# Regrouping the first feed-forward layer of a fp32-exact hybrid trunk: 18 of 22 chunks folded, and weight quarters loaded anew

## The chip, the core and the metric

The kernel runs on one core of one Trainium2 chip. The core has a matrix engine (TensorE, PE in the profile, with PEld for its weight loads), a vector engine (VectorE, DVE), a scalar engine (ScalarE, ACT), GpSimd (POOL) and SyncE (SP), which here issues most of the transfers from the chip's main memory. The metric is device microseconds of one execution; smaller is better.

## What is computed

512 tokens of width 1024 go through two layers in fp32. Layer 0 mixes tokens with gated linear attention (GLA), layer 1 with a gated DeltaNet (GDN). Behind each mixer stands a gated feed-forward ("ConvFFN"), which this change is about. Each sublayer ends with `x = LayerNorm(alpha * x + f(x))`. The feed-forward is, in short:

```
up   = x @ w_in                      # 1024 -> 2 * 2816: gate half and value half
up   = causal_dwconv(up, conv_w)     # width 3 along the tokens
f(x) = (gelu(gate) * value) @ w_out  # 2816 -> 1024
```

The inner width 2816 is 22 chunks of 128 columns.

## The kernel before

**Products.** Every fp32 operand is split into a high part (a cast to the matrix engine's fp32r format) and a low part (the difference); a product is then three matmuls, high by high, high by low and low by high, which accumulate in a PSUM bank. The splitting is done by `split_out` (L690): the cast mostly on ACT, the difference on DVE.

**Up-projection ("fm").** Each chunk gives two items, gate and value; an item is one weight tile of 128 columns, 8 input chunks by 3 parts = 24 matmuls of 512 columns. The evacuation is the convolution: one pass of ACT (L978) and two of DVE (L980), then gelu on ACT for the gate or a multiply on DVE for the value.

**Down-projection.** It goes in groups of chunks, `GROUPS = ((0, 8), (8, 16), (16, 22))`, each directly behind the up-projection of its chunks. The first two groups are folded (function `folded`). A fold takes a pair of chunks by both halves of the model width by two halves of the 512 tokens as a 2x2 block product and does it with seven block products in place of eight: `FORMS` names the seven combinations of the activations (made on DVE in a tile `form`, then split into `fh` and `fl`), and the names b11, b21, t1, t2, b22, t3, t4 are the seven combinations of the weights' quarters. One weight item holds a name for two pairs (128x1024). Each name takes 2 halves x 3 parts = 6 matmuls of 512 columns per pair. A pair is thus 42 matmuls. In the plain form (`out_rows`, tile `tm`), two chunks by two width halves by four blocks of 128 tokens by 3 parts are 48. The last group of six chunks is plain, token block by token block, because each block of tokens is followed by its LayerNorm.

**Weights of a fold.** `fold_load` (L384) loads the quarters b11, b12 and b22 into tiles `b` (six of them, tag "folded") which stay for the whole fold, and b21 into the pool of three `raw` tiles. `issue_fold` makes the sums in place on DVE (L395): t1 = b11 + b12, t2 = t1 + b22, and so on; t3 = b12 + b22 is made in the b12 tile. SP issues each load as soon as its tile is free, in the order of the plan. Split weights go into a pool of four tiles `wh` and four `wl`.

**LayerNorm between the layers (`ln`, L834 to L875).** For each block of 128 tokens: the plain rows are added to the residual `h` (L638, DVE, once for each half of the width), statistics are taken (L639), the root is made on ACT, four tiny DVE operations follow, one half is normalised on DVE (L858) and the other on ACT (L857); PE transposes both halves (`xT`, 4 transposes each), ACT applies gain and bias in eight pieces (L867), and the result is split into `xh` (DVE at L871 for half 0, ACT at L874 for half 1) and `xl` (DVE, L875). The next layer's matmuls need the `xh` and `xl` of its tokens: in the first items after the feed-forward, of two token blocks at a time.

**Order.** All work is issued by a Python planner into the engines' queues. Each engine runs its queue in order. Weights are asked for a number of items ahead (`look`), and small generators such as `ln` are pushed between matmuls by a cost model of the planner.

**Names for the steps below.** `form` is a tile of 2048 columns of which two exist; `fh`/`fl` are four pairs of 1792 columns; in the last group these and the six "folded" tiles are reused as 36 pieces ("parts") for the plain group's activations and split weights.

Of the kernel before, what the change touches and what calls it, by code (L numbers as in the profile page):

```python
# [15 lines left out]
P = 128  # L16
# [12 lines left out]
            "t4": ("a22", 0)}  # L29
FOLD_NEW = {"b11": "b11", "t1": "b12", "t2": "b22", "b21": "b21", "t3": None, "b22": None, "t4": "b21"}  # L30
FOLD = [(n, FOLD_NEW[n], *FOLD_ALL[n]) for n in ("b11", "b21", "t1", "t2", "b22", "t3", "t4")]
GATED = (("b11", "a11", 0), ("b21", "a12", 1), ("t1", "w1", 1), ("t2", "v2", 0), ("b22", "v4", 1), ("t3", "v3", 0),
         ("t4", "a22", 0))
GATED_NEW = {"b11": "b11", "b21": "b21", "t1": "b12", "t2": "b22", "b22": "b22", "t3": "b11", "t4": "b21"}
# [32 lines left out]
def blk(i, n=P):  # L67
    return slice(i * n, i * n + n)


class Trunk:
# [190 lines left out]
    def plan_fold(self, w, f0, f1):  # L262

        group = {"w": w, "f0": f0, "m": (f1 - f0) // 2}
        for name, quarter, _, _ in FOLD:
            for i in range(0, group["m"], 2):
                self.plan.append(("fold", group, name, quarter, i))

# [99 lines left out]

    def fold_load(self, group, quarter, i):


        w, m = group["w"], group["m"]
        n = min(2, m - i)
        if quarter == "b21":
            t = self.rp.tile([P, 1024], F32, name=self.uid("raw"), tag="raw")
        else:
# [6 lines left out]
        group[quarter, i] = t  # L385

    def issue_fold(self, group, name, quarter, i):
        nc = self.nc
        n = min(2, group["m"] - i)
        cols = slice(0, n * S)  # L390
        get = lambda q: group[q, i]
        t = get({"b21": "b21", "t3": "b12", "b22": "b22"}.get(name, "b11"))
        other = {"t1": "b12", "t2": "b22", "t3": "b22", "t4": "b21"}.get(name)
        if other:
            nc.vector.tensor_add(t[:, cols], t[:, cols], get(other)[:, cols])  # L395
            self.vec(0.62 * n)
        self.held += 1
        wh = self.wp.tile([P, 1024], F32R, name=self.uid("wh"), tag="wh")
        wl = self.wp.tile([P, 1024], F32R, name=self.uid("wl"), tag="wl")
        self.split_out(wh[:, cols], wl[:, cols], t[:, cols])  # L400
        self.vec(0.62 * n)
        return [(wh[:, blk(j, S)], wl[:, blk(j, S)]) for j in range(n)]

    def gated_load(self, group, name, i):
# [4 lines left out]
        else:  # L409
            t = self.rp.tile([P, 1024], F32, name=self.uid("raw"), tag="raw")  # L410
        quarter = GATED_NEW[name]
        col = group["col"] + (2 - int(quarter[2])) * S
# [7 lines left out]
    def issue_gated(self, group, name, i):  # L420
        nc = self.nc
        t = group.pop((name, i))
# [11 lines left out]
        self.vec(1.24)  # L434
# [3 lines left out]
        self.split_out(wh, wl, t)  # L438
        self.vec(1.24)
        return [(wh[:, blk(j, S)], wl[:, blk(j, S)]) for j in range(2)]  # L440

# [10 lines left out]
    def load_ahead(self, until):  # L452
# [3 lines left out]
        while self.loaded < min(len(self.plan), until) and self.plan[self.loaded][0] in ("fold", "gated"):  # L456
            if self.plan[self.loaded][0] == "gated":
                self.gated_load(*self.plan[self.loaded][1:])
            else:
                _, group, _, quarter, i = self.plan[self.loaded]  # L460
                if quarter:
                    self.fold_load(group, quarter, i)
            self.loaded += 1
# [384 lines left out]
    def ln(self, tb, spill=False):  # L848
# [12 lines left out]
        for hf in range(2):  # L861
# [7 lines left out]
            xs = (slice(None), slice(4 * hf, 4 * hf + 4), blk(tb))  # L869
            if hf == 0:  # L870
                nc.vector.tensor_copy(self.xh[xs], c4(xf))  # L871
# [83 lines left out]

    def ffn_plan(self, w_in, w_out):
        for f0, f1 in GROUPS:
            for f in range(f0, f1):
# [24 lines left out]
    def ffn(self, cw, li, g, b, final, out=False):  # L983
        nc = self.nc
        self.stage(f"ffn{li}", FFN_SLOTS)
        fine = lambda: tuple(self.mp.tile([P, 1792], F32R, name=self.uid(n), tag=n, bufs=4) for n in ("fh", "fl"))
        for gi, (f0, f1) in enumerate(GROUPS):
            act, items, forms = {}, [], []
            last = gi == len(GROUPS) - 1
            if last:  # L990
                self.parts = [t[:, blk(i, S)] for _ in range(4) for t in fine() for i in range(3)]
                for _ in range(FOLDED):
                    t = self.mp.tile([P, 1024], F32, name=self.uid("b"), tag="folded", bufs=FOLDED)
                    self.parts += [t[:, blk(i, S)].bitcast(F32R) for i in range(2)]
            for f in range(f0, f1):
# [39 lines left out]
            if last:  # L1035
                self.drain()
                self.ln_begin(li, g, b)
                if out:
                    t = self.mp.tile([P, 2048], F32, name=self.uid("form"), tag="form", bufs=2)
                    self.ln_gb([t[:, blk(i, S)] for i in range(4)])  # L1040
# [6 lines left out]
    def folded(self, forms, first):  # L1047
# [5 lines left out]
        banks = [[self.psum("fold") for _ in range(2)] for _ in range(3)]  # L1053
        uses = [[n for n, _, _, at in FOLD if at == i] for i in range(3)]
        fresh = {(tb, hf) for tb in range(NTB) for hf in range(2)} if first else set()
# [16 lines left out]
        self.look = 3  # L1072
        for name, _, form, at in FOLD:
            f = FORMS.index(form) * 256
# [847 lines left out]
def kernel(  # L1922
# [24 lines left out]
    t.gdn_plan(gdn_w_in[0], gdn_w_out[0])  # L1947
    t.ffn_plan(ffn_w_in[1], ffn_w_out[1])
    t.hd = t.dp.tile([S, D], F32, name="hd", tag="hd")
# [45 lines left out]
```

## Time and profile before

| | |
|---|---|
| median of 3 runs | 1230.29 us (1230.27 to 1231.0) |
| profiled execution, its own time | 1230.9 us |
| its span, first to last instruction | 1229.2 us |
| PE busy | 1222.5 us (99%) |
| DVE busy | 933.8 us (76%) |
| ACT busy | 604.4 us (49%) |
| moved by DMA | 133.67 MB, mean 109 GB/s |

The first feed-forward lies at about 223 to 572 us of the span, the second at about 875 us to the end. In the first, the fold of chunks 0 to 7 runs at 307 to 347 us, that of chunks 8 to 15 at 433 to 472 us, and the plain rows at 537 to 572 us. In the profile's rows, `fm` is up-projection (and the mixers' input projections), `fold` is a folded down-projection, `tm` a plain one. `out<-in` names tiles without numbers.

### The profile page before, as it was taken

Reading aid. Unit: us, or ns where it says so; the run is one execution under the profiler, and the core shown is the slowest. Engines: PE = TensorE matmul, PEld = TensorE weight load, DVE = VectorE, ACT = ScalarE, POOL = GpSimd, SP = SyncE. Lnnn points to the kernel's source line nnn. Section 1 sums busy time; section 2 is a strip of 40 time slices with the busy share of each in tenths; the row PEclk is TensorE's granted clock in tenths of the full one; section 3 lists DMA queues with packets and bytes.
Section 4 is the critical chain, followed back from the end, with each engine's and each line's share of the span. In section 5 each row is a group of like instructions: output and inputs, shape, how many; then the busy total and the mean of one; then the engine's idle time right before and its main releaser. Section 6 shows DMA issues by size and latency. Waiting matters only on the chain.

```text
span 1229.2 us, 17198 instructions
## 1 busy us (share of the span) xinstructions
PE 1222.5 (99%) x6554; PEld 1030.8 (84%) x6554; DVE 933.8 (76%) x1535; ACT 604.4 (49%) x1070; POOL 123.1 (10%) x159
## 2 busy tenths in 40 slices
PE   9999999999999999999999999999999999999998
PEld 8888888988888888888988888988988888888886
DVE  4966986689957895666779975688589966796667
ACT  5654764544434443454678555634644434443440
POOL 4000000071000000001152030200053000000000
PEclk9999999999999999999999999999999999999999
DMA  7432253442453213433344351244352262223321
GB/s 207 117 104 69 86 170 105 144 132 69 131 160 92 63 59 115 118 103 106 97 136 128 97 135 42 77 130 138 120 154 70 69 204 87 88 83 103 105 67 69
DMA packets 171186, 133.67 MB, mean 109 GB/s; under 512 B 16390, under 2 KB 140362, under 8 KB 171104
## 3 DMA queue, kind: packets, MB, share of 16 engines
q1 hardware_dynamic: 166272, 123.62, 34.0%
q0 software_dynamic: 3872, 8.30, 2.2%
q8 instruction: 51, 0.84, 0.3%
q10 hardware_dynamic: 960, 0.66, 0.2%
q14 instruction: 31, 0.25, 0.1%
HBM read 126.77 MB, written 5.78 MB: 108 GB/s over the span
## 4 chain that ended last, share of the span: by engine, by line
PE 99%; DVE 1%; ACT 0%; issue 0%; DVEq 0%; POOL 0%; ACTq 0%; POOLq 0%
PE fm L205 54%; PE tm L205 20%; PE fold L205 15%; PE o L205 2%; PE xT L223 1%; PE pq L205 1%; PE pg L205 1%; PE vn L205 1%; PE yT L223 1%; PE V L205 0%; PE s L205 0%; PE qs L205 0%; PE ks L205 0%; PE ds L205 0%; PE sa L205 0%; PE warm L764 0%
## 5 line engine op out<-in xcount | busy, mean ns | idle before, releaser
L205 PE MATMUL fm<-xh,wh 128*128 128x512 f32 (+2 forms) x1104 | 401.8, 366 | 0.7 <-ACT xh L690 0.7
L205 PE MATMUL fm<-xl,wh 128*128 128x512 f32 (+2 forms) x1104 | 399.9, 365 | 0.0
L205 PE MATMUL fm<-xh,wl 128*128 128x512 f32 (+1 forms) x1080 | 392.8, 366 | 0.0
L690 DVE TENSOR_TENSOR wl<-raw,wh 128x1024 fp32r<-128x1024 f32 (+1 forms) x162 | 201.0, 1243 | 152.6 <-ACT wh L690 152.3
L690 ACT CAST wh<-raw 128x1024 fp32r<-128x1024 f32 (+1 forms) x163 | 168.8, 1037 | 226.4 <-PE fm L205 143.7
L205 PEld LDWEIGHTS fm<-xh,wh 128*128 128x128 f32 (+1 forms) x1104 | 206.9, 188 | 33.8 <-ACT xh L690 1.1
L205 PEld LDWEIGHTS fm<-xl,wh 128*128 128x128 f32 (+1 forms) x1104 | 206.9, 188 | 32.7
L205 PEld LDWEIGHTS fm<-xh,wl 128*128 128x128 f32 x1080 | 202.8, 189 | 33.0
L980 DVE SCALAR_TENSOR_TENSOR conv<-fm,ffn_cw,conv 128x511 f32<-128x511 f32 x112 | 83.5, 745 | 8.6 <-ACT conv L978 7.2
L205 PE MATMUL fold<-wh,fh 128*128 128x512 f32 x224 | 87.6, 391 | 0.0
L205 PE MATMUL fold<-wl,fh 128*128 128x512 f32 x224 | 87.4, 390 | 0.1
L205 PE MATMUL fold<-wh,fl 128*128 128x512 f32 x224 | 87.2, 389 | 0.0
L690 ACT CAST wh<-b 128x1024 fp32r<-128x1024 f32 x48 | 49.6, 1053 | 60.4 <-PE fold L205 25.5
L998 ACT ACTIVATE conv<-conv 128x512 f32<-128x512 f32 x44 | 27.8, 632 | 80.5 <-DVE conv L980 80.5
L890 POOL TENSOR_TENSOR h<-h,gb 128x512 f32<-128x512 f32 x16 | 28.1, 1776 | 334.5 <-DMA gb<-in_ln_g_dram 334.5
L690 DVE TENSOR_TENSOR wl<-b,wh 128x1024 fp32r<-128x1024 f32 x48 | 57.9, 1220 | 2.3 <-ACT wh L690 2.3
L1511 DVE SCALAR_TENSOR_TENSOR conv<-fm,gdn_cw,conv 128x511 f32<-128x511 f32 (+2 forms) x72 | 54.0, 790 | 3.2 <-ACT conv L1509 2.6
L205 PE MATMUL tm<-wh,xh 128*128 128x512 f32 x128 | 52.9, 414 | 0.0
L205 PEld LDWEIGHTS fold<-wh,fh 128*128 128x128 f32 x224 | 42.0, 188 | 9.8 <-DVE h L1069 1.2
L205 PE MATMUL tm<-wh,xl 128*128 128x512 f32 x128 | 50.2, 392 | 0.0
L205 PE MATMUL tm<-wl,xh 128*128 128x512 f32 x128 | 50.0, 391 | 0.0
L205 PEld LDWEIGHTS fold<-wl,fh 128*128 128x128 f32 x224 | 42.0, 188 | 9.4 <-DVE wl L690 0.9
(358 smaller groups left out, 1965.5 us busy)
## 6 DMA issues: line engine op xcount, KB each, us to landing
raw<-in_ffn_w_in_dram SPq DMA_DIRECT2D x88, 512.0 KB, 3.9
raw<-in_gdn_w_in_dram SPq DMA_DIRECT2D x32, 512.0 KB, 4.1
raw<-in_ffn_w_out_dram SPq DMA_DIRECT2D x28, 512.0 KB, 3.7
raw<-in_gla_w_in_dram SPq DMA_DIRECT2D x26, 512.0 KB, 3.7
b<-in_ffn_w_out_dram SPq DMA_DIRECT2D x24, 512.0 KB, 4.9
raw<-in_gla_w_out_dram SPq DMA_DIRECT2D x8, 512.0 KB, 3.9
raw<-in_gdn_w_out_dram SPq DMA_DIRECT2D x8, 512.0 KB, 4.0
h<-in_x_dram SPq DMA_DIRECT2D x8, 256.0 KB, 4.3
```

Source lines behind the costliest of these rows:

```text
L205: t = self.nc.tensor.matmul(out, a, b, start=start, stop=stop, skip_group_check=joined)
L223: t = self.nc.tensor.transpose(out, a, self.ident[:n, :n])
L690: return self.nc.scalar.copy(dst_h, src), self.nc.vector.tensor_sub(dst_l, src, dst_h)
L890: nc.gpsimd.tensor_mul(h[hf], h[hf], gb[hf])
L980: nc.vector.scalar_tensor_tensor(a[:, d:], ps[:, :S - d], tap(2 - d), a[:, d:], ALU.mult, ALU.add)
L998: nc.scalar.activation(a, a, AF.Gelu)
L1511: self.conv = nc.vector.scalar_tensor_tensor(a[:, d:], ps[:, :S - d], tap(3 - d), a[:, d:], ALU.mult, ALU.add)
```

## The change

- `GROUPS` becomes a table by layer. The first feed-forward has groups (0, 8), (8, 18), (18, 22): 18 chunks folded and four plain. The second keeps (0, 8), (8, 16), (16, 22).
- The six "folded" tiles are gone. Each of the seven names loads its own quarter when it is due: b11, and b22 of the first two pairs, into `gw` (4 tiles), the other ones into `raw` (3 tiles); where a group has an odd pair, its single-pair items go into small slots `fq`. So b11, b12 and b22 are loaded twice in a fold. The weights' sums are no longer taken from kept quarters: the first item of a pair, b11, becomes the running total in `gw`; t1 and t2 add into it, t3 is the total less the reloaded b11 and is made in `raw`, and t4 adds the reloaded b21 to the total. The same function (`issue_quarter`, adds at L402, L405 and L407) now serves the gated stage of the GLA layer, whose t4 is made in the total too, where it was made in `raw`.
- `form` has one tile, not two; `fh`/`fl` have five pairs, not four. The pieces for the plain group are 30, not 36; in the second feed-forward what does not fit is put into the six slots of the stage.
- In `ln` the cast of half 0 goes from DVE to ACT for token blocks 0, 1 and 2, in all three places where `ln` runs between layers. Block 3 keeps it on DVE.

The core of the diff (the group of `GATED` names, the unchanged lines and the moved `gated_load` are left out):

```diff
-FOLD_NEW = {"b11": "b11", "t1": "b12", "t2": "b22", "b21": "b21", "t3": None, "b22": None, "t4": "b21"}
+QUARTERS = {"b11": "b11", "b21": "b21", "t1": "b12", "t2": "b22", "b22": "b22", "t3": "b11", "t4": "b21"}
...
-GROUPS = ((0, 8), (8, 16), (16, 22))
+GROUPS = {False: ((0, 8), (8, 18), (18, 22)), True: ((0, 8), (8, 16), (16, 22))}
...
-FOLDED = 6
+PAIRS = 5
...
-    def fold_load(self, group, quarter, i):
+    def fold_load(self, group, name, i):
...
-        if quarter == "b21":
-            t = self.rp.tile([P, 1024], F32, name=self.uid("raw"), tag="raw")
+        if name == "b11" or name == "b22" and i == 0:
+            t = self.mp.tile([P, 1024], F32, name=self.uid("gw"), tag="gw", bufs=4)
+        elif n == 1:
+            t = self.slot("fq")
         else:
-            t = self.mp.tile([P, 1024], F32, name=self.uid(quarter), tag="folded", bufs=FOLDED)
+            t = self.rp.tile([P, 1024], F32, name=self.uid("raw"), tag="raw")
...
-        get = lambda q: group[q, i]
-        t = get({"b21": "b21", "t3": "b12", "b22": "b22"}.get(name, "b11"))
-        other = {"t1": "b12", "t2": "b22", "t3": "b22", "t4": "b21"}.get(name)
-        if other:
-            nc.vector.tensor_add(t[:, cols], t[:, cols], get(other)[:, cols])
...
         elif name == "t3":
             nc.vector.tensor_sub(t, total, t)
         elif name == "t4":
-            nc.vector.tensor_add(t, total, t)
-            del group["sum", i]
+            nc.vector.tensor_add(total, total, t)
+            t = group.pop(("sum", i))
...
-            if hf == 0:
+            if hf == 0 and tb == NTB - 1:
                 nc.vector.tensor_copy(self.xh[xs], c4(xf))
...
-        fine = lambda: tuple(self.mp.tile([P, 1792], F32R, name=self.uid(n), tag=n, bufs=4) for n in ("fh", "fl"))
+        fine = lambda: tuple(self.mp.tile([P, 1792], F32R, name=self.uid(n), tag=n, bufs=PAIRS) for n in ("fh", "fl"))
...
-                        t = self.mp.tile([P, 2048], F32, name=self.uid("form"), tag="form", bufs=2)
+                        t = self.mp.tile([P, 2048], F32, name=self.uid("form"), tag="form", bufs=1)
...
-        for name, _, form, at in FOLD:
+        for name, form, at in FOLD:
```

Three places show how instructions move. In them a name's number tells tiles apart; `h_99` and `h_100` are the two halves of token block 0, `h_101` and `h_102` of block 1, `h_103` and `h_104` of block 2, `h_105` and `h_106` of block 3. Line numbers of the changed kernel are lower by 1 on PE (L204 for L205, L222 for L223), and by 8 in much of the rest (L682 for L690, L630 for L638, L867 for L875).

PE in the plain rows of the first feed-forward, where the transposes of token block 0 stand. Before:

```order
L205 MATMUL tm_4611<-fl_4081,fl_4083 128x512
L205 MATMUL tm_4611<-fh_4082,b_4087 128x512 x3
L223 MATMUL xT_4631<-ident_86,h_99 128x128 x4
L223 MATMUL xT_4643<-ident_86,h_100 128x128 x4
L205 MATMUL tm_4663<-fl_4083,fh_4076 128x512 x3
L205 MATMUL tm_4663<-b_4084,fh_4076 128x512 x2
```

And now:

```order
L204 MATMUL tm_4712<-fh_4337,fl_4338 128x512
L204 MATMUL tm_4712<-fl_4338 128x512
L222 MATMUL xT_4719<-ident_86,h_99 128x128 x4
L222 MATMUL xT_4731<-ident_86,h_100 128x128 x4
L204 MATMUL tm_4712<-fh_4337,fl_4338 128x512
L204 MATMUL tm_4774<-fl_4332,fh_4331 128x512 x3
```

Before, they stood behind the third half row (`tm_4611` is block 1's first half), with 18 matmuls to a half row; now they stand ahead of the last of the 12 matmuls of the fourth half row (`tm_4712`, block 1's second half).

PE at the end of the same rows, with the transposes of block 2 (`h_103`, `h_104`) and the GDN layer's first matmuls (`fm`). Before:

```order
L205 MATMUL tm_4825<-b_4084,fl_4077 128x512
L223 MATMUL xT_4832<-ident_86,h_103 128x128 x4
L223 MATMUL xT_4844<-ident_86,h_104 128x128 x4
L205 MATMUL tm_4825<-b_4085,fl_4077 128x512 x3
L205 MATMUL tm_4825<-b_4086,fh_4078 128x512 x3
L205 MATMUL tm_4825<-b_4088,fh_4082 128x512 x2
L205 MATMUL tm_4825<-b_4088,fl_4083 128x512
L205 MATMUL tm_4825<-b_4089,b_4087 128x512 x3
L205 MATMUL fm_4913<-xh,wh_4659 128x256
```

And now:

```order
L222 MATMUL xT_4840<-ident_86,h_101 128x128 x4
L222 MATMUL xT_4852<-ident_86,h_102 128x128 x4
L204 MATMUL tm_4832<-fl_4334,fl_4338 128x512
L204 MATMUL tm_4874<-fh_4335,fh_4331 128x512 x4
L204 MATMUL tm_4874<-fl_4336,fh_4331 128x512
L204 MATMUL tm_4874<-fh_4335,fl_4332 128x512
L204 MATMUL tm_4874<-fh_4337,fl_4336 128x512 x3
L204 MATMUL tm_4874<-fh_4337,fl_4338 128x512
L204 MATMUL tm_4874<-fl_4338 128x512
L204 MATMUL tm_4874<-fh_4337,fl_4338 128x512
L222 MATMUL xT_4930<-ident_86,h_103 128x128 x4
L222 MATMUL xT_4942<-ident_86,h_104 128x128 x4
```

Between the transposes of blocks 1 and 2 there stand 13 plain matmuls now, where there were 36, and block 2's transposes come behind the last plain row, ahead of the first `fm`.

DVE ahead of block 2's normalisation (the last row of each piece makes `h_103`), from the add of block 2's second half. Before:

```order
L638 TENSOR_TENSOR h_104<-h_104,tm_4735 128x512
L875 TENSOR_TENSOR xl<-xf_4759,xh 128x4x128
L639 BN_STATS ln_st_773_4708<-h_104 128x6
L690 TENSOR_TENSOR wl_4800<-raw_4797,wh_4799 128x1024
L834 BN_AGGR ln_mv_4782<-ln_st_773_4708 128x2
L838 TENSOR_SCALAR ln_var_4786<-ln_mv_4782 128x1
L842 RECIPROCAL ln_rs_4788<-ln_root_4784 128x1
L843 SCALAR_TENSOR_TENSOR ln_t_4789<-ln_rs_4788,ln_var_4786 128x1
L844 SCALAR_TENSOR_TENSOR ln_rs_4788<-ln_t_4789,ln_rs_4788 128x1
L856 SCALAR_TENSOR_TENSOR ln_nb_4793<-ln_mv_4782,ln_rs_4788 128x1
L858 TENSOR_SCALAR h_103<-h_103,ln_mv_4782,ln_rs_4788 128x512
```

And now, from the statistics behind that add:

```order
L631 BN_STATS ln_st_797_4775<-h_104 128x6
L682 TENSOR_TENSOR wl_4829<-raw_4826,wh_4828 128x1024
L826 BN_AGGR ln_mv_4811<-ln_st_797_4775 128x2
L630 TENSOR_TENSOR h_105<-h_105,tm_4832 128x512
L830 TENSOR_SCALAR ln_var_4815<-ln_mv_4811 128x1
L834 RECIPROCAL ln_rs_4817<-ln_root_4813 128x1
L631 BN_STATS ln_st_812_4833<-h_105 128x6
L835 SCALAR_TENSOR_TENSOR ln_t_4818<-ln_rs_4817,ln_var_4815 128x1
L867 TENSOR_TENSOR xl<-xf_4845,xh 128x4x128
L836 SCALAR_TENSOR_TENSOR ln_rs_4817<-ln_t_4818,ln_rs_4817 128x1
L848 SCALAR_TENSOR_TENSOR ln_nb_4822<-ln_mv_4811,ln_rs_4817 128x1
L850 TENSOR_SCALAR h_103<-h_103,ln_mv_4811,ln_rs_4817 128x512
```

The add and the statistics of block 3's first half and one `xl` now stand inside the chain that makes block 2's normalisation.

More of the change, by code (lines that the diff above doesn't have):

```diff
@@ L437, in issue_gated, with gated_load @@
         wl = self.wp.tile([P, 1024], F32R, name=self.uid("wl"), tag="wl")
-        self.split_out(wh, wl, t)
-        self.vec(1.24)
-        return [(wh[:, blk(j, S)], wl[:, blk(j, S)]) for j in range(2)]
+        self.split_out(wh[:, cols], wl[:, cols], t)
+        self.vec(0.62 * n)
+        return [(wh[:, blk(j, S)], wl[:, blk(j, S)]) for j in range(n)]
+    def gated_load(self, group, name, i):
+        if name == "b11":
+            t = self.mp.tile([P, 1024], F32, name=self.uid("gw"), tag="gw", bufs=2)
+        else:
+            t = self.rp.tile([P, 1024], F32, name=self.uid("raw"), tag="raw")
+        quarter = QUARTERS[name]
+        col = group["col"] + (2 - int(quarter[2])) * S
+        c0 = 2 * i + int(quarter[1]) - 1
+        src = group["w"].rearrange("(c p) f -> p c f", p=P)[:, c0:c0 + 3:2, col:col + S]
+        load = self.nc.sync.dma_start(t.rearrange("p (j f) -> p j f", j=2), src)
+        if name == "b11":
+            self.behind(load, self.load)
+        group[name, i] = t
+    def issue_gated(self, group, name, i):
+        return self.issue_quarter(group, name, i, 2)
     def prefetch(self):
@@ L459, in load_ahead @@
             else:
[L460 to L462 removed]
+                self.fold_load(*self.plan[self.loaded][1:])
             self.loaded += 1
```

65 lines of the change are left out of this document (21 added, 44 removed).

## The prediction

> **What bounds the kernel now.** I read first the page's head with the busy times and the clock, then the waits of PE, then the chain of work that ended last, then single stretches. The page:
>
> ```profile
> span 1229.2 us, 17198 instructions
> PE 1222.5 (99%) x6554; PEld 1030.8 (84%) x6554; DVE 933.8 (76%) x1535; ACT 604.4 (49%) x1070; POOL 123.1 (10%) x159
> PEclk9999999999999999999999999999999999999999
> PE 99%; DVE 1%; ACT 0%; issue 0%; DVEq 0%; POOL 0%; ACTq 0%; POOLq 0%
> ```
>
> PE is busy for all but 6.7 us of the span (1229.2 less 1222.5), the clock is granted in full in all 40 slices, and the chain that ended last runs through PE for 99%. All of PE's named waits (engine and line, what released it, total, times, longest):
>
> ```profile
> PE warm L764 <- POOL one L97: 1.1, 1, 1.1
> PE fm L205 <- ACT xh L690: 0.7, 1, 0.7
> PE mid L205 <- ACT diag L906: 0.6, 1, 0.6
> ```
>
> So the time is the matmul stream. A matmul that goes saves its pitch; anything else costs only where it makes PE wait. But a busy PE here may also be a PE whose matmul was held a little, so I compare each stretch of the chain with its count times the free pitch. Chain, start, length, what:
>
> ```profile
> 346.72 86.59 PE fm L205 x382
> 433.30 32.64 PE fold L205 x144
> 466.40 5.61 PE fold L205 x24
> 307.68 19.27 PE fold L205 x85
> 326.97 13.69 PE fold L205 x59
> 341.11 5.61 PE fold L205 x24
> ```
>
> Both 86.59 / 382 and 32.64 / 144 are 0.2267 us: the free pitch of 512 columns. The second fold of the first feed-forward (433.30) is thus at full rate but for its last 24, which take 5.61 in place of 5.44. The first fold (307.68) is at full rate up to 326.97; there 59 matmuls take 13.69 in place of 13.38, so 0.3 us are lost at that place.
>
> **The change, part by part.**
>
> *Matmuls.* A pair of chunks is 42 matmuls folded and 48 plain. One pair changes sides: 6 x 0.2267 = 1.36 us less. There is no doubt about the count; it is 0.11% of the time. One measurement can tell about 0.2% (2.46 us) from no change.
>
> *Transfers and the reload chain.* Before, each quarter came once; now three come twice, 512 KB for two pairs. For eight chunks that is 6 loads, 3 MB, on four folds some 13 MB beside the 133.67 MB at a mean of 109 GB/s. The queue has room. What matters is the three `raw` buffers: 11 of a fold's 14 items now pass through them. These are the rows for one load of such a quarter (times, KB, median us to landing) and for DVE's work in the first fold:
>
> ```profile
> raw<-in_ffn_w_out_dram SPq DMA_DIRECT2D x28, 512.0 KB, 3.7
> b<-in_ffn_w_out_dram SPq DMA_DIRECT2D x24, 512.0 KB, 4.9
> 303.19 1.22 DVE L395 TENSOR_TENSOR b<-b,b 128x1024 f32<-128x1024 f32 x1
> 308.05 1.22 DVE L395 TENSOR_TENSOR b<-b,b 128x1024 f32<-128x1024 f32 x1
> 324.56 1.22 DVE L395 TENSOR_TENSOR b<-b,raw 128x1024 f32<-128x1024 f32 x1
> 325.69 2.35 DVE L690 TENSOR_TENSOR wl<-b,wh 128x1024 fp32r<-128x1024 f32 x2
> L690 ACT CAST wh<-raw 128x1024 fp32r<-128x1024 f32 (+1 forms) x163 | 168.8, 1037 | 226.4 <-PE fm L205 143.7
> 312.00:337.00 25.00, 24.98 (x110) 20.33 (x110) 24.97 (x31) 10.76 (x11) 0.00 (x0) 1.00 0.41 129
> ```
>
> The last row is the stretch 312 to 337 us: length, then busy time of PE, PEld, DVE, ACT and POOL, the clock, the DMA share, GB/s. DVE is full there, and PE's lost 0.3 us at 326.97 is the first of the two `wl` that start at 325.69, which ends at 326.9. A buffer's turn is the load 3.7, an add 1.13 (324.56 to 325.69), the ACT cast 1.04 and the `wl` 1.18 (half of 2.35): 7.05 us. Three buffers give an item every 2.35 us; PE takes one in 12 x 0.2267 = 2.72. So the loads keep pace as long as they land within 3 x 2.72 less 3.35 = 4.8 us. Singly issued loads are the row with 3.7; the 4.9 belongs to `b` tiles issued in a run while the queue is fullest, and the reloads are issued singly, each when DVE frees a buffer. I take 3.7: no stall.
>
> *The adds of a fold* stay eight for eight chunks. But the two b12 + b22 (303.19 and 308.05), which were made ahead of the fold, become "total less b11" inside it. Ahead of the `wl` at 325.69 there is then one add less net, 1.13 us, which is more than the 0.3 lost there; behind it the t3 and t4 items have less cover, about 1 us on my count of the queue. The first folds of both feed-forwards can gain 2 x 0.3 = 0.6. Bounds: -0.6, and +2.0 if two such items in each of the four folds come 0.25 us late. I take -0.3.
>
> *The fold of ten* has 21 items of 12 or 6 matmuls, 210 x 0.2267 = 47.6 us. Its DVE load per matmul is that of the second fold, which ran at 0.2267 throughout. The updates of `h` are as many as before. 0.
>
> *One `form` tile, five pairs.* The next pair's value convolution on ACT must wait until DVE has split the last one's form (128x1792, a single operation of 2 us); PE meanwhile has weights two items ahead, 2 x 24 x 0.2267 = 10.9 us of matmuls. 0.
>
> *The plain rows of the first feed-forward.* This is the place of the main cost. Before, chain and DVE groups of 536.7 to 572.4 us (times, busy us, mean ns), then some single rows of DVE and ACT:
>
> ```profile
> 536.83 12.48 PE tm L205 x54
> 549.31 0.95 PE xT L223 x8
> 550.27 9.56 PE tm L205 x42
> 559.83 0.87 PE xT L223 x8
> 568.88 0.87 PE xT L223 x8
> 569.76 2.77 PE tm L205 x12
> L639 DVE BATCH_NORM_STATS2 ln_st<-h 128x6 f32<-128x512 f32 x7 | 4.9, 694 | 0.2
> L690 DVE TENSOR_TENSOR wl<-raw,wh 128x1024 fp32r<-128x1024 f32 x4 | 4.8, 1208 | 0.0
> L638 DVE TENSOR_TENSOR h<-h,tm 128x512 f32<-128x512 f32 x7 | 4.8, 686 | 3.1 <-PE tm L205 3.1
> L875 DVE TENSOR_TENSOR xl<-xf,xh 128x512 fp32r<-128x512 f32 x5 | 3.5, 691 | 0.5 <-ACT xh L874 0.4
> L871 DVE CAST xh<-xf 128x512 fp32r<-128x512 f32 x3 | 1.3, 425 | 1.9 <-ACT xf L867 1.9
> 555.75 1.21 DVE L690 TENSOR_TENSOR wl<-raw,wh 128x1024 fp32r<-128x1024 f32 x1
> 556.88 0.20 DVE L834 BATCH_NORM_AGGREGATE ln_mv<-ln_st 128x2 f32<-128x12 f32 x1
> 558.24 0.54 DVE L858 TENSOR_SCALAR h<-h,ln_mv,ln_rs 128x512 f32<-128x512 f32 x1
> 552.73 0.62 ACT L874 CAST xh<-xf 128x512 fp32r<-128x512 f32 x1
> ```
>
> Before, PE loses some 0.4 us here: 54 matmuls at 0.2267 are 12.24, not 12.48, and three smaller differences. A block of tokens gives PE 36 matmuls and two transposes, 8.16 + 0.87 = 9.0 us; with four chunks it is 24 and two, 5.44 + 0.87 = 6.3. DVE's work for a block hardly shrinks: two adds and two statistics, 4 x 0.61 (a large operation starts 0.08 us ahead of the end of the one in front: 555.75 + 1.21 against 556.88); aggregate to normalisation 1.36 (556.88 to 558.24) and 0.54; two `xl` 1.22; one to two `wl` of the GDN weights at 1.13. With one that is 6.7 us of pure work, less some 0.25 us of waiting for the root into which other work now falls: 6.5 against PE's 6.3, before DVE waits once for PE. The cast that goes to ACT (0.42 from DVE, 0.62 onto ACT) helps and leaves the balance near zero.
>
> Following the new order row by row with these durations, from the end of the last `fm`: the transposes of block 0 stand behind 47 matmuls (10.65 us), but the normalisation is done at about 11.1: 0.4 us of wait. For block 1, PE comes 36 matmuls and one pair of transposes later, and DVE has two `wl`, two `xl`, three adds and three statistics to do in between, the first only when PE's interrupted half row is done: 0.5 us. For block 2, PE comes 13 matmuls and the transposes later, 2.95 + 0.87 = 3.8 us; DVE has statistics, `wl`, aggregate, add, statistics, `xl` and the tiny ones first (0.61 + 1.13 + 0.24 + 3 x 0.61 + 0.9 = 4.7) and 0.54 for the normalisation, 5.2 in all, about 0.3 of which passes while PE waits for block 1's second half on ACT: 1.1 us. Together 2.0 us, less the 0.4 lost before: +1.6. Bounds: -0.4 (none of these waits, and the old one gone) and +4 (each of three blocks late by a further `wl` and a half `xl`, some 0.8 us). If they stand, the next that is late are block 1's `xl` of half 1, which the first GDN matmuls need about 0.4 us after it is made.
>
> The Trainium skill says in VectorE: DVE Perf Modes, section on the DRAIN you can't avoid, that the next operation does not start before the pipeline of the last one has emptied. Read strictly, the 0.08 us of overlap would be gone, with some 16 large operations in these three chains 1.3 us more, and the sum below would come to 1231.5. The trace doesn't agree with that reading: 556.88 lies ahead of 555.75 + 1.21 = 556.96.
>
> *Start of these rows.* With all GDN weights cast ahead on ACT, the last chunk's convolution starts up to one cast (1.04) later; the new order puts 20 matmuls, 4.5 us, ahead of the first that needs it, and I find the two about equal. 0, bounds 0 and +0.8.
>
> *The same cast in the other two places where `ln` runs between layers:* a block there has 24 matmuls too and PE has no gap; the last operand comes about 0.5 us later with over 1 us to spare. 0. *Second feed-forward's tail and the GLA gated stage:* the operands move to other tiles, nothing joins the last chain. 0, at most 0.3 either way.
>
> **Sum:** -1.36 - 0.3 + 1.6 = -0.1 us. On the profiled execution (1230.9, span 1229.2) that is 1230.8; that execution lies 0.6 above the median of 1230.29, so against the median it is 1230.2.
>
> **Rivals.**
>
> *A: the saving alone arrives.* The planner's order hides the three waits, because DVE runs a little ahead (in the old rows it waited 3.1 us for `tm`, which is slack that I may have undercounted). Then -1.36 - 0.6 and at most the old 0.4: 1228.3 to 1228.0. For it speaks that no PE wait of this sort was named in the old trace; against it that PE's share of a block falls by 2.7 us and DVE's by 0.4.
>
> *B: the reloads come late (slower).* Place: t3 and t4 of each fold, five `raw` items in a row. Above a landing of 4.8 us each item is late by a third of the excess. At 6.0 us that is 0.4 x 5 x 4 folds = 8 us, less the cover of 1 us in each fold: +4, 1234.2. For it speak the 4.9 of the `b` row and a DMA share of 0.41 in the first fold; against it the 3.7.
>
> *C: the plain rows cost more.* Every block is DVE-bound by two `wl` in place of one; the upper end of +4: 1232.6.
>
> *D: the change does next to nothing,* because gain and cost cancel: that is the forecast itself.
>
> **Chances.** Forecast (waits of 0.8 to 2.5 us in the plain rows) 0.52; A 0.22; B 0.12; C 0.14. Below 1227.8 (faster by over 0.2%) only a quarter of A reaches, where other small holds go as well: 0.06. Above 1232.8 lie B and half of C: 0.19. Within 0.2%: 0.75. The range takes in A's value and C's: 1228.0 to 1233.2; it leaves out B and the ends of A and C.
>
> **What would show it.** In the new profile, `tm` and `fold` matmuls fall and rise by 48 and 42. In the chain, the plain rows of the first feed-forward would show pieces of `xT` with waits of DVE's normalisation (L850) ahead of them, in the order 0.4, 0.5, 1.1 us; without them A holds. The folds would each take 38.1 us at 0.2267, without the loss at the ninth item; if PEld waits for `wl` there, or DVE's adds wait for `raw`, B holds. I would be wrong altogether if PE waited in the fold of ten or ahead of a convolution for the single `form`.

## The result, and the profile after

| | before | after |
|---|---|---|
| median | 1230.52 us (7 runs, 1230.27 to 1231.18) | 1234.49 us (7 runs, 1233.58 to 1235.35) |
| profiled execution, its span | 1230.9, 1229.2 us | 1233.58, 1231.6 us |

The ratio is 1.003, 95% interval 1.002 to 1.004: the change costs 4.0 us, 0.32%, and the kernel's own runs spread over 1.8 us where they spread over 0.9 before. 1234.49 lies above the range of 1228.0 to 1233.2.

The page of the changed kernel: PE has 6 matmuls less and 1.0 us less busy time, and still the span is 2.4 us longer. What the chain of waits passes through has changed most.

```profile
span 1231.6 us, 17277 instructions
PE 1221.5 (99%) x6548; PEld 1028.8 (84%) x6548; DVE 936.7 (76%) x1536; ACT 611.2 (50%) x1081; POOL 122.0 (10%) x159
DMA packets 176003, 142.84 MB, mean 116 GB/s; under 512 B 16727, under 2 KB 140699, under 8 KB 175921
PE 81%; DVE 13%; issue 2%; ACT 2%; DMA 1%; DVEq 0%; ACTq 0%; POOL 0%; POOLq 0%
```

The DMA line says how much was really loaded anew: 142.84 less 133.67 is 9.2 MB, not the 13 MB of the prediction. Of the four quarters, b21 was loaded twice before the change as well, once for its own item and once for t4, and b12 still comes once. Only b11 and b22 come a second time now, so a fold of eight chunks has 14 loads of 512 KB where it had ten. (The text on the change, which says that b11, b12 and b22 are loaded twice, has this wrong.)

Before, 99% of that chain was PE. Now 13% of it is DVE and 1% is waiting for loads. PE's waits (engine and line, releaser, total, times, longest) name two new ones, besides one of 0.2 us:

```profile
PE fold L204 <- DVE h L1058: 2.2, 4, 0.8
PE xT L222 <- DVE h L850: 0.6, 1, 0.6
```

The first is new: inside the folds PE waits for DVE's update of `h`, since that update must have read the PSUM bank before the next name may write into it. How it comes to be late is read in DVE's timeline of the first fold (start, length, operation, and in brackets the idle time before it with its releaser):

```profile
327.19 2.35 DVE L682 TENSOR_TENSOR wl<-raw,wh 128x1024 fp32r<-128x1024 f32 x2
329.46 1.28 DVE L1056 SCALAR_TENSOR_TENSOR h<-h,fold 128x512 f32<-128x512 f32 x2
330.65 1.22 DVE L405 TENSOR_TENSOR raw<-gw,raw 128x1024 f32<-128x1024 f32 x1
333.27 1.23 DVE L407 TENSOR_TENSOR gw<-gw,raw 128x1024 f32<-128x1024 f32 x1 [1.40 <-DMA raw<-in_ffn_w_out_dram]
334.41 0.68 DVE L1058 TENSOR_TENSOR h<-h,fold 128x512 f32<-128x512 f32 x1
335.01 1.22 DVE L682 TENSOR_TENSOR wl<-raw,wh 128x1024 fp32r<-128x1024 f32 x1
```

And SP's issues of the loads in the same stretch:

```profile
318.09 4.97 SPq L385 DMA_DIRECT2D raw<-in_ffn_w_out_dram  x2
326.70 0.37 SPq L385 DMA_DIRECT2D gw<-in_ffn_w_out_dram  x1
328.43 1.50 SPq L385 DMA_DIRECT2D raw<-in_ffn_w_out_dram  x2
```

The quarter for t4 is issued at 328.43, the moment that the first of the two `wl` at 327.19 frees a `raw` buffer. It lands at 333.2. DVE would have been free for its add (L407) at 331.87 and stands still for 1.40 us; the update of `h` and the `wl` of t3's second item queue behind that add. PE then waits for them.

This load is not one of the new ones. Before, t4's quarter went into a `raw` buffer too, but only four of a fold's ten loads used those buffers, and it was issued at 290.51, 34 us ahead of its add (the row at 324.56 in the prediction):

```profile
290.51 0.37 SPq L384 DMA_DIRECT2D raw<-in_ffn_w_out_dram  x1
```

Now 11 of 14 loads go through the three buffers, and the same load leaves 3.4 us ahead of the moment at which DVE wants it. From the chain of the first fold and of the second feed-forward's first fold:

```profile
328.43 4.81 DMA raw<-in_ffn_w_out_dram
982.40 4.57 DMA raw<-in_ffn_w_out_dram
```

And PE's timeline at both ends of these two folds (the first matmul of the fold, the first `fm` behind it):

```profile
306.69 0.39 PE L204 MATMUL fold<-wh,fh 128*128 128x512 f32 x1
346.38 0.39 PE L204 MATMUL fm<-xh,wh 128*128 128x512 f32 x1
960.68 0.39 PE L204 MATMUL fold<-wh,fh 128*128 128x512 f32 x1
1000.11 0.39 PE L204 MATMUL fm<-xh,wh 128*128 128x512 f32 x1
```

That is 39.7 and 39.4 us for 168 matmuls, which at 0.2267 us take 38.1. Before, the second feed-forward's first fold lost its time in the same two pieces as the first one's, which the prediction shows:

```profile
978.77 13.67 PE fold L205 x59
992.89 5.61 PE fold L205 x24
```

Laid beside the chain of before, stretch by stretch, each less its matmuls at 0.2267 us (two `fm` matmuls that stood inside each fold before are taken off too) and its transposes at 0.87 us for a block:

| stretch | lost before | lost after | change |
|---|---|---|---|
| first feed-forward, first fold | 0.5 | 1.6 | +1.1 |
| its second fold (8 chunks, then 10) | 0.2 | 1.1 | +0.9 |
| its plain rows, from the last `fm` to the first of GDN | 0.4 | 1.6 | +1.2 |
| second feed-forward, first fold | 0.5 | 1.3 | +0.9 |
| second feed-forward, second fold | 0.2 | 0.1 | -0.1 |
| matmuls saved | | | -1.4 |

(The changes are taken before rounding.) That is +2.6. The span grew by 2.4, in an execution that reached the first feed-forward 0.8 us earlier than that of before (222.84 against 223.66 us) and lost some 0.5 us in GDN and at the end. No part of the change accounts for the 0.8: it is there already at 51.13 against 51.90 us, ahead of the first stage that was changed. The profiled execution is the fastest of the seven; the median run lost 0.9 us more.

The other two places: the end of the fold of ten, and the plain rows, in the chain:

```profile
455.34 39.45 PE fold L204 x174
494.88 0.63 ACT wh L682
495.53 0.69 DVE wl L682
496.22 0.61 DVE h L1058
496.97 7.08 PE fold L204 x30
```

174 matmuls at 39.45 are the free pitch; then PE waits for an update of `h` (L1058) which stands in DVE's queue behind a `wl`, which waits for ACT's cast of it.

```profile
558.75 1.07 PE xT L222 x8
559.82 8.21 PE tm L204 x36
572.49 1.09 PE xT L222 x8
```

Block 0's transposes take 1.07 in place of 0.87, block 1's follow without a wait, and those of block 2 begin at 572.49 behind the 0.6 us wait for the normalisation (L850).

### The profile page after: what moved, and what is told of

It is laid out like the page before. It is cut to its first block, busy times and chain, and to the rows that moved or that the text cites. A ratio compares the mean times of both kernels' runs of the same rounds, so it can differ in the third digit from the quotient of the medians.

```text
span 1231.6 us, 17277 instructions
## 1 busy us (share of the span) xinstructions
PE 1221.5 (99%) x6548; PEld 1028.8 (84%) x6548; DVE 936.7 (76%) x1536; ACT 611.2 (50%) x1081; POOL 122.0 (10%) x159
## 2 busy tenths in 40 slices
DMA packets 176003, 142.84 MB, mean 116 GB/s; under 512 B 16727, under 2 KB 140699, under 8 KB 175921
## 4 chain that ended last, share of the span: by engine, by line
PE 81%; DVE 13%; issue 2%; ACT 2%; DMA 1%; DVEq 0%; ACTq 0%; POOL 0%; POOLq 0%
PE fm L204 43%; PE tm L204 18%; PE fold L204 10%; DVE wl L682 4%; PE o L204 2%; DVE conv L972 1%; DVE form L972 1%; ACT wh L682 1%; DVE fl L682 1%; DMA raw<-in_ffn_w_out_dram 1%; PE xT L222 1%; DVE form L998 1%; DVE gw L402 1%; PE pq L204 1%; PE pg L204 1%
## 5 line engine op out<-in xcount | busy, mean ns | idle before, releaser
L204 PE MATMUL fm<-xh,wh 128*128 128x512 f32 (+2 forms) x1104 | 401.9, 366 | 0.7 <-ACT xh L682 0.7
L204 PE MATMUL fm<-xl,wh 128*128 128x512 f32 (+2 forms) x1104 | 399.9, 365 | 0.0
L204 PE MATMUL fm<-xh,wl 128*128 128x512 f32 (+1 forms) x1080 | 392.9, 366 | 0.0
L682 DVE TENSOR_TENSOR wl<-raw,wh 128x1024 fp32r<-128x1024 f32 (+1 forms) x172 | 212.8, 1241 | 144.0 <-ACT wh L682 142.4
L682 ACT CAST wh<-raw 128x1024 fp32r<-128x1024 f32 (+1 forms) x173 | 179.4, 1038 | 240.0 <-PE fm L204 150.2
L204 PEld LDWEIGHTS fm<-xh,wh 128*128 128x128 f32 (+1 forms) x1104 | 206.9, 188 | 33.6 <-ACT xh L682 0.9
L204 PEld LDWEIGHTS fm<-xl,wh 128*128 128x128 f32 (+1 forms) x1104 | 207.0, 188 | 32.7
L204 PEld LDWEIGHTS fm<-xh,wl 128*128 128x128 f32 x1080 | 202.8, 189 | 32.8
L204 PE MATMUL fold<-wh,fh 128*128 128x512 f32 x238 | 93.2, 391 | 2.3 <-DVE h L1058 2.2
L204 PE MATMUL fold<-wl,fh 128*128 128x512 f32 x238 | 92.9, 390 | 0.0
L204 PE MATMUL fold<-wh,fl 128*128 128x512 f32 x238 | 92.2, 389 | 0.0
L972 DVE SCALAR_TENSOR_TENSOR conv<-fm,ffn_cw,conv 128x511 f32<-128x511 f32 x108 | 80.6, 746 | 9.9 <-ACT conv L970 8.2
L682 ACT CAST wh<-gw 128x1024 fp32r<-128x1024 f32 (+1 forms) x48 | 48.5, 1016 | 69.4 <-PE fm L204 18.4
L682 DVE TENSOR_TENSOR wl<-gw,wh 128x1024 fp32r<-128x1024 f32 (+1 forms) x48 | 56.1, 1175 | 4.1 <-ACT wh L682 4.0
L204 PEld LDWEIGHTS fold<-wh,fh 128*128 128x128 f32 x238 | 44.7, 188 | 13.7 <-issue 2.4
L204 PE MATMUL tm<-wh,xh 128*128 128x512 f32 x128 | 52.9, 413 | 0.0
L204 PEld LDWEIGHTS fold<-wl,fh 128*128 128x128 f32 x238 | 44.7, 188 | 9.7 <-DVE wl L682 0.6
L204 PEld LDWEIGHTS fold<-wh,fl 128*128 128x128 f32 x238 | 44.7, 188 | 9.3
L972 DVE SCALAR_TENSOR_TENSOR form<-fm,ffn_cw,form 128x511 f32<-128x511 f32 x68 | 50.7, 746 | 1.5 <-ACT form L970 0.4
```

The lines of the kernel that those rows point to most:

```text
L204: t = self.nc.tensor.matmul(out, a, b, start=start, stop=stop, skip_group_check=joined)
L682: return self.nc.scalar.copy(dst_h, src), self.nc.vector.tensor_sub(dst_l, src, dst_h)
L972: nc.vector.scalar_tensor_tensor(a[:, d:], ps[:, :S - d], tap(2 - d), a[:, d:], ALU.mult, ALU.add)
```

## The experiments

Two theories at the start. R: the reloaded quarters go through three `raw` buffers, come late and hold DVE, whose queue is in order. D: DVE is simply full in the folds, and the two additions that moved into them are the cost; the loads only happen to be last.

**1. The t4 load left out.**

```diff
         w, n = group["w"], min(2, group["m"] - i)
+        if name == "t4":
+            group[name, i] = group["sum", i] if ("sum", i) in group else group["b11", i]
+            return
```

> The kernel after, but the reload for t4 (quarter b21) is left out in all folds of both feed-forwards: t4 adds the running total to itself, so the output is not the reference's; every DVE, ACT and PE operation stays. Theory R (reloads through three raw buffers come late and hold DVE, which works in order): the losses at the end of the first folds (1.1 us in the first feed-forward, 0.9 in the second) and of the fold of ten (about 1.1) go for the most part, 1231.5 to 1232.5 us. Theory D (DVE is simply full there, the two adds that moved into the fold are the cost): the loads do not matter, 1234 to 1235 us as the kernel after.

Measured: 1230.68 us, ratio to before 0.9998 (0.9989 to 1.0007). Both first folds run at the free pitch, without even the old loss of 0.5; all DVE work is still there:

```profile
307.40 38.19 PE fold L204 x168
959.50 38.18 PE fold L204 x168
496.01 7.09 PE fold L204 x30
```

D has fallen: the same operations on DVE cost nothing without the load. The wait at the end of the fold of ten (496.01; 454.40 + 39.45 is 493.85, and six more matmuls take 1.4) stays at 0.8 us, so it is not one of the loads, other than I had expected. The time lies below the 1231.5 to 1232.5 of theory R all the same: more went with the load than the 2.0 us of the profiled execution.

**2. One item taken out of the `raw` buffers ahead of t3 and t4,** with all loads kept.

```diff
-        if name == "b11" or name == "b22" and i == 0:
+        if name == "b11" or name == "b22" and n == 2:
```

> The kernel after, but both items of b22 are loaded into gw, which takes one item out of the raw buffers just ahead of t3 and t4; same loads, same work. Theory R: the t4 loads are issued some 2.5 us earlier in each fold of eight, so the first folds lose at most 0.3 us each: 1232 to 1233 us. Theory D: as the kernel after, 1234 to 1235 us. If the next group's b11, which now waits for a gw buffer, blocks the queue, slower than the kernel after.

Measured: 1230.91 us, ratio to before 1.0000 (0.9991 to 1.0009), 3.6 us below the changed kernel. DVE's timeline of the first fold:

```profile
330.74 1.22 DVE L405 TENSOR_TENSOR raw<-gw,raw 128x1024 f32<-128x1024 f32 x1
331.88 1.22 DVE L407 TENSOR_TENSOR gw<-gw,raw 128x1024 f32<-128x1024 f32 x1
```

SP's issues show why: the second load of the pair at 318.18, some 4.6 us behind the first, is now t4's, 9 us ahead of its add.

```profile
318.18 4.97 SPq L385 DMA_DIRECT2D raw<-in_ffn_w_out_dram  x2
326.79 2.10 SPq L385 DMA_DIRECT2D gw<-in_ffn_w_out_dram  x2
306.98 38.19 PE fold L204 x168
958.94 38.18 PE fold L204 x168
```

(The last two rows are the chain's first folds.) The next group's b11 now waits for a `gw` buffer and blocked nothing. Theory R holds: the same bytes and the same work, and the whole excess over before is gone. Its time, 1232 to 1233, was too high: the gain of 3.6 in the medians is larger than the folds' 2.7 in the profiled executions (they lost 1.6 and 1.3 and now lose 0.1 and 0.1), and the eleventh run below shows where some of the rest may lie.

**3. The groups of before, all else as after.**

```diff
-GROUPS = {False: ((0, 8), (8, 18), (18, 22)), True: ((0, 8), (8, 16), (16, 22))}
+GROUPS = {False: ((0, 8), (8, 16), (16, 22)), True: ((0, 8), (8, 16), (16, 22))}
```

> The kernel after with the groups of before in the first feed-forward too (16 chunks folded, 6 plain): reloads, one form tile and the cast on ACT stay. Theory R with the regrouping as a second cost: the 1.36 us of saving goes, the losses of the fold of ten (1.1) and of the plain rows (1.2) go too, the first folds' 2.0 stay: 1232 to 1233 us. If the regrouping is the whole cost: 1230.5 us. If the reloads are the whole cost and the regrouping a gain: 1235 to 1236 us.

Measured: 1241.41 us, ratio 1.0087 (1.0073 to 1.0101). None of the three. PE has a wait that no other kernel has, at the first GDN matmuls:

```profile
PE fm L204 <- ACT xh L866: 5.4, 1, 5.4
573.31 0.25 ACT xf L859
579.56 7.39 PE fm L204 x43
```

(The rows under the wait are of the chain.) Six plain chunks need 36 pieces; with 30 the last six lie in the stage's slots, and `ln` needs those slots for its `xf`. The first `xf` runs at 573.3, behind the last plain row; before, it ran during the rows. So the edit brought in a loss of its own and says nothing on what the regrouping costs by itself; the sixth run does that. One thing it does show: with the groups of before the first fold still takes 39.7 us from its first matmul (307.49) to the next `fm` (347.15), so its loss does not need the regrouping. It also shows why the group of six could not stay as it was once the kept quarters were gone.

**4. The cast of half 0 back on DVE.**

```diff
-            if hf == 0 and tb == NTB - 1:
+            if hf == 0:
```

> The kernel after with the cast of half 0 on DVE again in the layer norms. If DVE is what is late in the plain rows of the first feed-forward, its 0.42 us for each block adds to the waits there: 0.3 to 1.0 us slower than the kernel after, 1235 to 1235.5. If ACT is what is late there (its 0.62 us more for each block), 0.5 us faster. The other two places stay without a wait.

Measured: 1235.41 us, 0.9 above the changed kernel; ratio to before 1.0037 (1.0024 to 1.0050). The wait for block 2's normalisation grows from 0.6 to 1.9 us:

```profile
PE xT L222 <- DVE h L850: 1.9, 1, 1.9
```

DVE is what is late in the plain rows, and the moved cast is a gain of about 1 us there. (The interval of the ratio overlaps that of the changed kernel; the wait carries the reading.)

**5. The kernel before with only that cast on ACT.**

```diff
-            if hf == 0:
+            if hf == 0 and tb == NTB - 1:
```

> The kernel before with nothing changed but the cast of half 0 on ACT for token blocks 0 to 2. If the cast is free either way where a block has 36 plain matmuls, 1230.5 to 1231 us, as before. If ACT's 0.62 us more makes the normalised rows late anywhere, 1231.5 to 1233.

Measured: 1230.74 us, ratio 0.9999 (0.9990 to 1.0009). With 36 plain matmuls to a block the cast is free on either engine.

**6. The regrouping alone undone, in the second run's kernel,** with room for six plain chunks.

```diff
-GROUPS = {False: ((0, 8), (8, 18), (18, 22)), True: ((0, 8), (8, 16), (16, 22))}
+GROUPS = {False: ((0, 8), (8, 16), (16, 22)), True: ((0, 8), (8, 16), (16, 22))}
-FFN_SLOTS = 6
+FFN_SLOTS = 7
...
+                if not out:
+                    t = self.mp.tile([P, 2048], F32, name=self.uid("form"), tag="form", bufs=1)
+                    self.parts += [t[:, blk(i, S)].bitcast(F32R) for i in range(4)]
```

> The second run's kernel (both b22 items in gw) with the groups of before in the first feed-forward, and room for its six plain chunks: the form tile's four pieces and a seventh slot, so that the layer norm finds its slots free. If the regrouping by itself costs as much as it saves (1.36 us of matmuls against 1 us at the end of the fold of ten and 1.2 us in the plain rows), 1229.8 to 1230.5. If the regrouping is a gain of its own, 1231.5 to 1232.5.

Measured: 1230.09 us, ratio to before 0.9996 (0.9987 to 1.0005). PE has none of the new waits, the transposes of all blocks take 0.87, the folds run free. Against the second run the regrouping thus costs some 0.7 us net: it saves 1.4 of matmuls and loses about 1.0 in the fold of ten and 1.0 in the plain rows (these stretches lose 1.1 and 1.3 in the second run, 0.1 and 0.3 here). The medians say the same, each beside the kernel before on its own chip: the second run lies 0.06 above it (1230.91 against 1230.85), this one 0.59 below (1230.09 against 1230.68). That difference is small beside the intervals; the stretches of the chain carry it.

**7. Fewer GDN weights split between the plain rows,** in the second run's kernel.

```diff
-                    self.look = min(WB, 2 * tb + hf - 2)
+                    self.look = min(WB, 2 * tb + hf - 2) if pieces == 2 or n > 4 else 1 + (2 * tb + hf > 6)
```

> The second run's kernel with fewer GDN weights split between the plain rows of the first feed-forward: none of the three differences wl stands ahead of the normalisations of blocks 1 and 2 (the planner moves the transposes along). If the plain rows are late because DVE has those wl in its queue, PE's waits there fall from about 1.6 to 0.5 us: 1229.6 to 1230.2. If the chain add, statistics, root, normalisation is itself what is late, or GDN's first items then wait for their weights: 1230.8 or more.

Measured: 1230.12 us, ratio to before 0.9993 (0.9985 to 1.0002). The wait on L850 is gone; the transposes of blocks 0, 1 and 2 in the chain of the plain rows:

```profile
557.44 1.08 PE xT L222 x8
565.59 0.88 PE xT L222 x8
569.20 0.87 PE xT L222 x8
```

Blocks 1 and 2 now come through at the free 0.87; block 0's 1.08 is untouched. The `wl` in DVE's queue are thus the likely cause of the largest wait there. It is not shown by this run alone: the planner moved the transposes of blocks 1 and 2 too (31 plain matmuls stand between blocks 0 and 1 and 12 between 1 and 2, where the second run has 36 and 13, and six come behind block 2), so order and load changed together.

**8. Weights asked two ahead, not three, in the fold of ten.**

```diff
-        self.look = 3
+        self.look = 3 - m % 2
```

> The second run's kernel with weights asked two items ahead, not three, in the fold of ten alone. In it DVE's update of h stands behind the difference wl of a single-pair item, which waits for ACT's cast, which waits for PE to free a weight tile. If that ring is the 0.8 to 1 us that PE loses there, it goes: 1229.8 to 1230.2. If the item's weight is simply late, it loses more: 1231 to 1233.

Measured: 1230.83 us, ratio 0.9998 (0.9989 to 1.0007); the wait of 0.8 us at the end of the fold of ten stays as it was. The new order still had the single-pair `wl` of t4 ahead of t3's update in DVE's queue, so the run did not take the ring apart that it was meant for, and tells neither way.

**9. The odd pair first in each name,** in the second run's kernel: the items of the fold of ten are one pair, two pairs, two pairs.

```diff
-            for i in range(0, group["m"], 2):
+            for i in self.starts(group["m"]):
...
+        return ([0] if m % 2 else []) + list(range(m % 2, m, 2))
```

> The second run's kernel (both b22 items in gw) with the odd pair of the fold of ten taken first in each name, not last. In the second run PE waits 0.8 us for DVE's update of t3, which stands in DVE's queue behind the difference wl of t4's single-pair item; that one waits for ACT's cast, and this for the weight tile that PE frees only at the start of t3's last item, a single pair of 1.36 us. With a full item of 2.72 us there, cast and difference (2.2 us) fit in front of the update. If that is the mechanism, the wait of 0.8 goes: 0.6 to 0.9 us less than the second run, about 1230.1. If it is the update's own length (0.7 us for each half), it stays.

Measured: 1230.36 us, ratio to before 0.9996 (0.9987 to 1.0004), some 0.5 below the second run, each beside the kernel before on its own chip, and so a little less than the 0.6 to 0.9 expected. The wait falls from 0.8 to 0.4 us, not to nothing. The chain at that place:

```profile
492.83 1.06 ACT wh L690
493.91 1.23 DVE wl L690
495.14 0.61 DVE h L1066
495.88 4.14 PE fold L204 x17
```

The ring is as described: cast, difference, update, then PE. But with a full item in it cast and difference take 2.3 us and the update 0.7, 3.0 and some delays between, against the item's 2.72: it shrinks and doesn't vanish.

**10. Runs 7 and 9 together.**

> The edits of the seventh and the ninth run together: both places where the regrouping lost time are mended, the 1.36 us of matmuls stay saved, and the first folds' old 0.3 us each are gone too. Sum from the kernel before: -1.4 - 0.6 + 0.4 = -1.6 us, 1228.8 to 1229.6, the fastest of all.

Measured: 1229.41 us (11 runs, 1229.08 to 1230.01), ratio to before 0.9989 (0.9980 to 0.9998). It is the fastest, and the only one whose interval lies below the kernel before, by 0.1%. It keeps the 18 folded chunks and the reloads.

**11. The changed kernel once more.**

> The changed kernel once more, beside the last two on the same chip: 1233.5 to 1235.5 us, and in its trace the t4 loads of the first folds land 4.5 to 4.9 us after their issue, as in its first trace.

Measured: 1234.24 us (6 runs, 1232.8 to 1234.9), ratio 1.0025 (1.0014 to 1.0036). In this profiled execution the t4 loads of the two first folds take:

```profile
328.60 4.87 DMA raw<-in_ffn_w_out_dram
983.59 4.78 DMA raw<-in_ffn_w_out_dram
```

The second feed-forward's first fold takes 40.6 us (from 960.89 to the `fm` at 1001.51), where it took 39.4 in the first trace. Only 0.2 of these 1.2 us are the landing (4.78 against 4.57). The other 1.0 lies ahead of the load: it is issued 22.7 us behind the fold's first matmul, and 21.7 in the first trace, because DVE, which frees its buffer, runs 1.0 us later. DVE fell behind some 56 us ahead of the fold, at one split of a `form` (two rows of this trace, then the same two of the first trace; a bracket is the idle time ahead of the row):

```profile
904.53 7.82 POOL L882 TENSOR_TENSOR h<-h,gb 128x512 f32<-128x512 f32 x4 [103.87 <-DMA gb<-in_ln_g_dram]
904.70 3.00 DVE L682 TENSOR_TENSOR fl<-form,fh 128x1792 fp32r<-128x1792 f32 x1
904.49 2.02 DVE L682 TENSOR_TENSOR fl<-form,fh 128x1792 fp32r<-128x1792 f32 x1
905.72 7.13 POOL L882 TENSOR_TENSOR h<-h,gb 128x512 f32<-128x512 f32 x4 [105.27 <-DMA gb<-in_ln_g_dram]
```

POOL applies the LayerNorm's gain and bias to the rows of `h` there, and while it does so DVE's operations take longer in all traces, that of before too (a `wl` 1.4 to 2.3 us, elsewhere 1.2). Here POOL started 0.2 us ahead of that `fl`, in the first trace 1.2 us behind its start, and the `fl` took 1.0 us more. In the ninth run's trace it is the same: POOL starts at 902.73, the `fl` at 903.00 takes 2.90, and that fold takes 39.1 us where the second run's takes 38.2. In the eleven other traces this `fl` takes 2.0. That may be why the runs of this kernel differ from each other; no run moved POOL's work alone.

## Why the prediction was wrong

- *Matmuls, -1.36:* right; counts and pitch are as forecast.
- *Transfers and the reload chain, "I take 3.7: no stall":* this is the step that failed, together with the -0.3 for the folds' adds. Its count of bytes was off (9.2 MB, not 13), but that is not what failed. Two other things were wrong in it. The landing of the loads that matter was 4.57 to 4.87 us, not 3.7: two of them and a `gw` load are issued within 3 us of each other. And the test was the wrong one. I compared a buffer's turn as a rate (7.05 / 3 = 2.35 against PE's 2.72). But a buffer isn't filled, used and freed at once: items are split only some three ahead of PE, so a landed quarter waits in its buffer, and the next load leaves only when DVE frees one. What counts is the lead of a single load: freed at 328.43, wanted by DVE at 331.87, 3.4 us. Even at 3.7 it would have been late by 0.3. The sign that I had named for late loads, DVE's adds waiting for `raw`, is there with 1.40 us. Measured in place of -0.3: +2.0 for the two first folds in the profiled execution, more in the median.
- *The adds of a fold, -0.3:* the old loss of 0.3 at the ninth item is indeed gone once the loads are in time (38.19 for 168 in run 2), which is the gain that the step spoke of; in the changed kernel it was buried under the late load.
- *Rival B* was this mechanism at this place, with 1234.2 as its time and a chance of 0.12. Its point of decision, a landing above 4.8 us, was set too high by the same error of rate for lead, and so its chance was set too low and the range left it out. That its time came within 0.3 of the measured one is chance: it counted five late items in each of four folds at a landing of 6.0 us, where one load in each of two folds was late enough for PE to feel it, and the other 2.1 us came at two places that B does not have. In the second folds DVE also waits for a t4 load, 0.9 and 0.3 us, and PE loses nothing by it (the fold of ten loses the same without that load, run 1).
- *The fold of ten, 0:* wrong, +0.9; a wait of PE there was the sign by which I would be wrong altogether. I argued from DVE's load for each matmul, but the loss is a ring at the single-pair item: PE frees a weight tile, ACT casts, DVE differences, and only then comes the update that PE waits for. Run 9 halves it by giving the ring a longer item.
- *The plain rows, +1.6:* the mechanism is right (run 4 shows that DVE is late, run 7 points to the `wl` in its queue), the size 0.4 too high. It was +1.2: block 2's wait 0.6 us and about 0.2 around it in place of 1.1, block 1 none in place of 0.5, block 0 0.2 in place of 0.4, and 0.3 at the rows' start, which I had costed at 0 to 0.8. With a size below the forecast, nothing in these rows calls for the strict reading of the Trainium skill's page VectorE: DVE Perf Modes (section The DRAIN you can't avoid), by which it would have been 1.3 larger still. The same section of the Trainium skill adds that a next operation that is not held starts earlier, and the traces agree: in the new one too, two `wl` of 1.22 us take 2.35 together (327.19).
- *Cast, `form`, five pairs, second tail, 0:* the cast is free in the kernel before (run 5) and a gain of 0.9 in the new plain rows (run 4). The single `form` and the five pairs are inside every kernel of runs 2 and 6, which lose nothing to be put down to them.
- *The GLA gated stage, 0:* right. From its first folded matmul to the first feed-forward the chain takes 102.8 us before (120.89 to 223.66) and 102.7 now (120.12 to 222.84).

Along the sum: -1.4 + 2.0 + 0.9 + 1.2 = 2.7 and not -0.1 in the profiled execution, and 4.0 in the medians. What stays open is why the loads land 4.6 to 4.9 us in some runs and places and 3.7 in others: the neighbours in the queue differ, but no run changed them alone.

## What to carry to other kernels

For a buffer ring, the rate of the ring is not the test: take one load, mark when its buffer is freed and when the first in-order engine will want it, and hold that lead against the slow end of the landing times, not their median. Where an engine works in order, a late operand costs whatever stands behind it in the queue, here an update that frees a PSUM bank. What moves into a ring can delay a load that was there before, so look at all loads of the ring and not at the new ones alone. Where a kernel is at 99% of one engine, a saving of 0.1% can be had only if every new wait is looked for at the places where an item got shorter: the halved item and the shorter rows each lost most of what the matmuls saved.

## What was not expected

The load that came late was not one that the change had added, but one that it had crowded. Taking one of the eleven items out of the three buffers gave 3.6 us, with not a byte and not an operation less. And where POOL's work on `h` began a little ahead of the split of a `form` and not behind its start, the fold that starts some 56 us on took about 1 us longer (runs 9 and 11).
